# Writing a relative-bias table to DRAM as 8 copies of each row instead of 128, and reading it back with sixteen loads of eight partitions

## The chip, the cores and the metric

One core of a Trainium2 chip runs the whole program. The metric is the device time of one execution in microseconds (us). The core's engines are TensorE (PE, with its weight loads listed apart as PEld), VectorE (DVE), ScalarE (ACT), GpSimd (POOL) and SyncE (SP). Each runs its own list of instructions in order and waits on semaphores. SP and POOL also issue DMAs: those of SP stand in the profile's queue q1, those of POOL in q0. Both queues' packets are carried by the same 16 DMA engines.

## The reference, cut to what matters

The program is a decoder trunk of two layers on 256 tokens of width 1024. A layer is a feed-forward half-step (gate, up, silu, down), a mixing step with three kinds of attention, and a second feed-forward half-step. Each step is modulated by vectors that come from a conditioning vector `c` and a large weight `w_ada`. All arithmetic is float32, and every weight matrix is read from HBM once.

What matters here is the bias that two of the attention kinds add to their scores. For each of 12 heads it depends only on the distance of query and key:

```python
def band_bias(table_cols, dilation):
    rel = jnp.arange(BLK)[:, None] + BLK - jnp.arange(2 * BLK)[None, :]
    b = t5_bucket(jnp.maximum(rel, 0) * dilation)
    return jnp.transpose(table_cols[b], (2, 0, 1)).astype(jnp.float32)
...
    s = jnp.einsum('nbqhgd,nbkhd->nbhgqk', qb, kk) * (Dh ** -0.5) + bias
```

So for a head, row p of the 128 x 256 bias block is the same vector of 383 distances, read from a start that moves one place to the left with each row: T[p, k] = row[127 - p + k].

## The kernel before, in words

**Order of the work.** The program is a list of units in an order fixed by hand: first feed-forward step (stage s=0), mixing step (s=1), feed-forward (s=2), and the same for the second layer (s=3 to 5). A unit is a piece of weight of 128 x 1024 float32. It is loaded into a `raw` tile of 1 MB that holds two units (L133, three such tiles), split by ACT into a high part `wH` (L150) and by DVE into a low part `wL` (L158), and then used by PE in three products for each piece: high x high, low x high, high x low (L594 for the products `pf`, `pq`, `pg`; L706 for the rows `pd` and `pe` of the down product). Six `wH` and six `wL` tiles exist. `feed()` prepares units up to five ahead of the one that PE is at.

**The modulation vectors.** Woven between the units is a second stream: `w_ada` pieces of 512 KB (tile `ada`, L260, two tiles), each multiplied by a scalar per partition and added to an accumulator `acc` (L281 on ACT for the first of eight, L283 on DVE for the others). Its pace per unit is set by the table `PACE`; the chunks that the next stage needs are completed at that stage's end. A load of a new piece is issued by SP only when the piece two before it has been consumed, and DVE runs the `acc` and `wL` instructions in one order.

**End of a feed-forward step.** The last four units of the down product are run half by half of the columns (L736 to L761); after each half DVE adds the result to `x` (`y` L535, `x` L536), then follow the mean square (`jk` L452), the root on POOL (`r` L466, L467), the scaled `xn` (L475) and the transposes `psn` (L488) that start the next stage. In the mixing step the first products are `pv` (L942).

**The bias table.** `bias_loads` (L413) fetches a one-hot matrix, a mask `mk` and the 32 x 12 table early in stage 0. `bias_table` (L425), called after unit 16 of that stage, makes `mk`, the 12 rows of 383 values, with one matmul (L428) and one DVE addition (L429). It stores them to DRAM as `row` (L431), and with a DMA from DRAM to DRAM writes each row 128 times into `scr` (L433). `load_bias` (L435), called at the start of each of the two mixing steps (L1149), reads from `scr` with one DMA the whole 128 x 12 x 256 tile `T` (in the profile `Tm`, since it lies in a larger tile of that name): the stride of 382 between partitions makes the moving start. T is first used at L1054, by the additions of the dilated heads.

Of the kernel before, what the change touches and what calls it, by code (L numbers as in the profile page):

```python
# [10 lines left out]
F32 = mybir.dt.float32  # L11
# [5 lines left out]
P = 128  # L17
# [6 lines left out]
NHEAD = 12  # L24
NDIST = 383
# [64 lines left out]
class Trunk:  # L90
# [334 lines left out]
    def bias_table(self):  # L425
        nc, oh, mk, rb = self.nc, self.oh, self.mk, self.rb
        p = self.ps("psr")
        nc.tensor.matmul(p[:NHEAD, :NDIST], rb, oh, start=True, stop=True)  # L428
        nc.vector.tensor_tensor(mk, p[:NHEAD, :NDIST], mk, op=ALU.add)  # L429
        row = self.dp.tile([NHEAD, NDIST], F32, tag="row", name="row")  # L430
        nc.gpsimd.dma_start(row, mk)  # L431
        self.scr = self.dp.tile([NHEAD, P, NDIST], F32, tag="scr", name="scr")
        nc.gpsimd.dma_start(self.scr, row.unsqueeze(1).to_broadcast([NHEAD, P, NDIST]))  # L433

    def load_bias(self, T):  # L435
        base = self.scr[:, 0:P, 0:256]
        src = bass.AP(tensor=base.tensor, offset=base.offset + P - 1,
                      ap=[[NDIST - 1, P], [P * NDIST, NHEAD], [1, 256]])
        self.nc.gpsimd.dma_start(T, src)


    def square(self, t, cols, tag):
# [908 lines left out]
```

## Time and profile before

| | |
|---|---|
| median of 3 runs | 1211.04 us (1210.54 to 1213.16) |
| the profiled execution | 1215.12 us, of which the span of its instructions is 1213.4 us |
| PE busy | 1181.0 us, 97% of the span |
| DVE busy | 837.3 us, 69% |
| ACT busy | 616.0 us, 51% |
| POOL busy | 19.0 us, 2% |
| moved by DMA | 287.55 MB, mean 237 GB/s |

The busy times say that PE has work at nearly every moment, but a matmul that waits inside its pipeline or runs at half clock counts as busy too. What matters for a change in the DMAs is where PE, and the chain of work that ends last, waits for data; that is read from the chain in order of time and from tables by stretch, which stand below the diff.

### The profile page before, as it was taken

To read this page: it belongs to the slowest core of one execution; us is meant where nothing else is said; L and a number is where in the kernel's file an instruction comes from. 1 tells how busy PE (TensorE), PEld (TensorE's weight loads), DVE (VectorE), ACT (ScalarE), POOL (GpSimd) and SP (SyncE) were. 2 spreads that over 40 slices of the span, in tenths; PEclk is the share of its full clock that TensorE was granted. 3 is DMA by queue.
4 is the path that set the end of the run, shared out by engine and by line. 5 is a ranking of instruction groups with operands and counts; after the bars stand their busy time and mean duration, and the time that the engine had idled before them with its cause. 6 is when DMAs were issued, how large, how long until landed. Compare 5 with 4: busy or idle time off the path is not lost.

```text
span 1213.4 us, 21101 instructions
## 1 busy us (share of the span) xinstructions
PE 1181.0 (97%) x8765; PEld 1102.9 (91%) x8765; DVE 837.3 (69%) x1087; ACT 616.0 (51%) x953; POOL 19.0 (2%) x38
## 2 busy tenths in 40 slices
PE   6999998899999999999999999999999999999997
PEld 5999986699999899999889999889999998999986
DVE  3677575878889888766577666567766788555544
ACT  5555343556555475444365444346655456444432
POOL 1000000000000000000000000000000000000000
PEclk9999999899999999999999999999999999999999
DMA  9999889698769959876738676748743584556550
GB/s 318 313 303 332 272 308 318 211 314 271 253 230 314 319 176 326 263 243 242 261 112 298 219 242 226 258 157 291 264 149 113 186 276 147 190 178 197 180 176 35
DMA packets 189671, 287.55 MB, mean 237 GB/s; under 512 B 6806, under 2 KB 155496, under 8 KB 189576
## 3 DMA queue, kind: packets, MB, share of 16 engines
q1 hardware_dynamic: 187656, 279.88, 68.8%
q0 software_dynamic: 1776, 6.14, 1.7%
q8 instruction: 68, 1.11, 0.4%
q14 instruction: 27, 0.22, 0.1%
q10 hardware_dynamic: 144, 0.20, 0.0%
HBM read 285.12 MB, written 3.42 MB: 238 GB/s over the span
## 4 chain that ended last, share of the span: by engine, by line
PE 85%; DMA 6%; DVE 3%; ACT 2%; issue 2%; POOL 1%; SPq 0%; POOLq 0%; ACTq 0%; DVEq 0%
PE pf L594 37%; PE pd L706 16%; PE pg L594 12%; PE pq L594 7%; DMA ada<-in_w_ada 5%; PE pb L594 3%; PE pf L624 3%; PE pv L942 2%; DVE acc L283 1%; DVE wL L158 1%; PE adaf L212 1%; DMA first<-in_w_ada 1%; PE psn L488 1%; ACT wH L150 1%; ACT jk L452 0%
## 5 line engine op out<-in xcount | busy, mean ns | idle before, releaser
L158 DVE TENSOR_TENSOR wL<-raw,wH 128x1024 fp32r<-128x1024 f32 (+1 forms) x384 | 461.8, 1211 | 224.8 <-ACT wH L150 224.3
L150 ACT CAST wH<-raw 128x1024 fp32r<-128x1024 f32 (+1 forms) x384 | 393.1, 1040 | 244.5 <-PE pd L706 90.1
L594 PE MATMUL pf<-hH,wH 128*128 128x256 f32 x1312 | 324.5, 285 | 0.4 <-DVE hH L505 0.4
L594 PE MATMUL pf<-hH,wL 128*128 128x256 f32 x1312 | 323.5, 284 | 0.0
L594 PEld LDWEIGHTS pf<-hH,wH 128*128 128x128 f32 x1312 | 253.1, 193 | 1.7 <-issue 0.9
L594 PEld LDWEIGHTS pf<-hH,wL 128*128 128x128 f32 x1312 | 253.5, 193 | 0.2 <-issue 0.2
L594 PE MATMUL pf<-hL,wH 128*128 128x256 f32 x1312 | 183.8, 283 | 0.0
L283 DVE SCALAR_TENSOR_TENSOR acc<-ada,sc,acc 128x1024 f32<-128x1024 f32 x112 | 143.4, 1280 | 40.6 <-DMA ada<-in_w_ada 40.6
L594 PEld LDWEIGHTS pf<-hL,wH 128*128 128x128 f32 x1312 | 169.1, 192 | 0.0
L706 PE MATMUL pd<-wL,ffH 128*128 128x512 f32 x336 | 132.7, 395 | 5.1 <-DVE wL L158 5.1
L706 PE MATMUL pd<-wH,ffH 128*128 128x512 f32 x336 | 132.5, 394 | 0.0
L706 PE MATMUL pd<-wH,ffL 128*128 128x512 f32 x336 | 132.2, 393 | 0.0
L594 PE MATMUL pg<-hH,wH 128*128 128x256 f32 x384 | 96.0, 288 | 0.0
L594 PE MATMUL pg<-hH,wL 128*128 128x256 f32 x384 | 94.0, 283 | 0.0
L652 ACT ACTIVATE sil<-pf 128x256 f32<-128x256 f32 x88 | 33.3, 382 | 98.4 <-PE pf L594 98.4
L706 PEld LDWEIGHTS pd<-wL,ffH 128*128 128x128 f32 x336 | 63.9, 190 | 19.3 <-DVE wL L158 6.2
L706 PEld LDWEIGHTS pd<-wH,ffH 128*128 128x128 f32 x336 | 63.9, 190 | 14.0 <-issue 0.8
L706 PEld LDWEIGHTS pd<-wH,ffL 128*128 128x128 f32 x336 | 64.0, 190 | 13.2
L594 PEld LDWEIGHTS pg<-hH,wH 128*128 128x128 f32 x384 | 73.5, 191 | 2.3 <-issue 0.9
L594 PEld LDWEIGHTS pg<-hH,wL 128*128 128x128 f32 x384 | 73.6, 192 | 0.0
L653 DVE TENSOR_TENSOR f<-pf,sil 128x256 f32<-128x256 f32 x88 | 36.9, 422 | 33.9 <-ACT sil L652 33.9
L594 PE MATMUL pq<-hH,wH 128*128 128x256 f32 x224 | 55.8, 287 | 0.0
(215 smaller groups left out, 1437.2 us busy)
## 6 DMA issues: line engine op xcount, KB each, us to landing
ada<-in_w_ada SPq DMA_DIRECT2D x128, 512.0 KB, 5.4
raw<-in_w_ffn_down SPq DMA_DIRECT2D x44, 1024.0 KB, 4.8
raw<-in_w_in SPq DMA_DIRECT2D x42, 1024.0 KB, 6.1
raw<-in_w_ffn_gate SPq DMA_DIRECT2D x41, 1024.0 KB, 6.1
raw<-in_w_ffn_up SPq DMA_DIRECT2D x41, 1024.0 KB, 5.8
first<-in_w_ada SPq DMA_DIRECT2D x32, 256.0 KB, 6.0
raw<-in_w_out SPq DMA_DIRECT2D x8, 1024.0 KB, 7.1
raw<-in_w_ffn_gate SPq DMA_DIRECT2D x12, 256.0 KB, 6.0
```

Source lines behind the costliest of these rows:

```text
L150: nc.scalar.copy(u.H, u.view(self.raw_tiles[u.raw]))
L158: nc.vector.tensor_tensor(u.L, u.view(self.raw_tiles[u.raw]), u.H, op=ALU.subtract)
L212: self.nc.tensor.matmul(self.first_ps[q % 2][32 * i:32 * i + 32, 0:P], w, src[:, i * P:(i + 1) * P], start=kb in (0, None), stop=kb == KB - 1)
L283: self.nc.vector.scalar_tensor_tensor(acc, src, sc, acc, ALU.mult, ALU.add)
L488: self.nc.tensor.transpose(p[:, i * P:(i + 1) * P], xn[:, fb * P:(fb + 1) * P], self.ident)
L594: nc.tensor.matmul(out, w[:, kb, cs], x[:, kb, :], start=i == 0, stop=i == n - 1)
L624: self.nc.tensor.matmul(ps[fb][:, S * up:S * up + S], w[:, 2 * k + up, b * P:(b + 1) * P], x[:, 2 * q + k, :], start=q == 0 and not up and ...
L652: nc.scalar.activation(sil, p[:, :S], AF.Silu)
L653: nc.vector.tensor_tensor(f32, p[:, S:], sil, op=ALU.mult)
L706: self.nc.tensor.matmul(out, x[:, kb, sl], w[:, 0, hs], start=first and i == 0, stop=last and i == 2)
L942: self.nc.tensor.matmul(out, x[:, 4 * (i % 2) + k, sl], w[:, k, :], start=i % 2 == 0 and j == 0, stop=i % 2 == 1 and j == n - 1)
```

## The change

The table `scr` gets 8 copies of each row instead of 128. They are written by eight DMAs straight from `mk` in SBUF, one for each copy, and the DRAM tile `row` with its store goes. T is read by sixteen DMAs of eight partitions each instead of one of 128: copy i serves partition r + i, and the start of each load moves with r. The same bytes of T arrive, 1.5 MB for each of the two mixing steps; all DMAs concerned are issued by POOL before and after. The lines below the edit move by two (L439 becomes L441, L1054 becomes L1056).

```diff
--- before.py
+++ after.py
@@ -427,16 +427,18 @@
         p = self.ps("psr")
         nc.tensor.matmul(p[:NHEAD, :NDIST], rb, oh, start=True, stop=True)
         nc.vector.tensor_tensor(mk, p[:NHEAD, :NDIST], mk, op=ALU.add)
-        row = self.dp.tile([NHEAD, NDIST], F32, tag="row", name="row")
-        nc.gpsimd.dma_start(row, mk)
-        self.scr = self.dp.tile([NHEAD, P, NDIST], F32, tag="scr", name="scr")
-        nc.gpsimd.dma_start(self.scr, row.unsqueeze(1).to_broadcast([NHEAD, P, NDIST]))
+        self.scr = self.dp.tile([NHEAD, 8, NDIST], F32, tag="scr", name="scr")
+        for r in range(8):
+            nc.gpsimd.dma_start(self.scr[:, r, :], mk)
 
     def load_bias(self, T):
-        base = self.scr[:, 0:P, 0:256]
-        src = bass.AP(tensor=base.tensor, offset=base.offset + P - 1,
-                      ap=[[NDIST - 1, P], [P * NDIST, NHEAD], [1, 256]])
-        self.nc.gpsimd.dma_start(T, src)
+
+
+        for r in range(0, P, 8):
+            base = self.scr[:, 0:8, 0:256]
+            src = bass.AP(tensor=base.tensor, offset=base.offset + P - 1 - r,
+                          ap=[[NDIST - 1, 8], [8 * NDIST, NHEAD], [1, 256]])
+            self.nc.gpsimd.dma_start(T[r:r + 8], src)
```

The order on POOL, from the table to the first read of T, before the change. `r` are the roots of the norms, and the names in brackets are the semaphores that a row waits for (DMASW0 to DMASW7 are the eight that POOL's DMAs take in turn, DMAHW0 to 7 those of SP's):

```order
L431 DMA row<-mk 12x383 [waits DVE_49]
L433 DMA scr<-row 1536x1x383 [waits DMASW3_49]
L466 TENSOR_TENSOR r_0_2311<-ms_0_2287 128x1 [waits DVE_49,Activation_49]
L467 TENSOR_TENSOR r_0_2311<-r_0_2311,mhalf 128x1 [waits Pool_49]
L467 TENSOR_TENSOR r_1_2427<-r_1_2427,mhalf 128x1 [waits DVE_49]
L439 DMA Tm_2485<-scr 128x12x256 [waits DMAHW3_49,DMAHW4_49,DMAHW2_49,DMAHW5_49,DMAHW1_49,DMAHW6_49,DMAHW0_49,DMAHW7_49,DMASW4_49,PE_49]
```

The same place after it; of the last eight loads of T the first two stand here, and the other six differ only in the semaphore's number:

```order
L432 DMA scr<-mk 12x383 [waits DVE_49]
L432 DMA scr<-mk 12x383 x4
L432 DMA scr<-mk 12x383 [waits DMASW0_49]
L432 DMA scr<-mk 12x383 [waits DMASW1_49]
L432 DMA scr<-mk 12x383 [waits DMASW2_49]
L468 TENSOR_TENSOR r_0_2316<-ms_0_2292 128x1 [waits DVE_49,Activation_49]
L469 TENSOR_TENSOR r_0_2316<-r_0_2316,mhalf 128x1 [waits Pool_49]
L469 TENSOR_TENSOR r_1_2432<-r_1_2432,mhalf 128x1 [waits DVE_49]
L441 DMA Tm_2490<-scr 8x12x256 [waits DMAHW0_49,DMASW7_49,DMAHW1_49,DMASW6_49,DMAHW2_49,DMASW5_49,DMAHW3_49,DMASW4_49,DMAHW4_49,DMASW3_49,DMAHW5_49,DMASW2_49,DMAHW6_49,DMASW1_49,DMAHW7_49,DMASW0_49,PE_49]
L441 DMA Tm_2490<-scr 8x12x256 x7
L441 DMA Tm_2490<-scr 8x12x256 [waits DMASW3_49]
L441 DMA Tm_2490<-scr 8x12x256 [waits DMASW4_49]
```

The wait of the copying DMA for `row` is gone, and no compute instruction of POOL has changed its place. Of the sixteen loads of T eight can be in flight; each of the others waits until an earlier one has landed and freed its semaphore.

On DVE the first use of T in the first mixing step stood as follows before, with one semaphore for T:

```order
L283 SCALAR_TENSOR_TENSOR acc_1_2889<-ada_3108,sc,acc_1_2889 128x1024 [waits DMAHW3_49,DVE_49]
L1054 SCALAR_TENSOR_TENSOR p_dil_3224<-pa_dil_3215,Tm_2485 128x2x256 [waits DMASW5_49,PE_49]
L1054 SCALAR_TENSOR_TENSOR p_dil_3224<-pb_dil_3216,Tm_2485 128x256
L1054 SCALAR_TENSOR_TENSOR p_dil_3224<-pc_dil_3217,Tm_2485 128x2x128 [waits PE_49]
L1054 SCALAR_TENSOR_TENSOR p_dil_3224<-pb_dil_3216,Tm_2485 128x128
```

And after the change, with eight:

```order
L283 SCALAR_TENSOR_TENSOR acc_1_2909<-ada_3128,sc,acc_1_2909 128x1024 [waits DMAHW3_49,DVE_49]
L1056 SCALAR_TENSOR_TENSOR p_dil_3244<-pa_dil_3235,Tm_2490 128x2x256 [waits DMASW4_49,DMASW3_49,DMASW5_49,DMASW2_49,DMASW6_49,DMASW1_49,DMASW7_49,DMASW0_49,PE_49]
L1056 SCALAR_TENSOR_TENSOR p_dil_3244<-pb_dil_3236,Tm_2490 128x256
L1056 SCALAR_TENSOR_TENSOR p_dil_3244<-pc_dil_3237,Tm_2490 128x2x128 [waits PE_49]
L1056 SCALAR_TENSOR_TENSOR p_dil_3244<-pb_dil_3236,Tm_2490 128x128
```

Its place among DVE's instructions is unchanged. The same eight semaphores in place of one are waited for at two instructions near the end of stage 0, a `y` (L535) and the second half of an `xn` (L478), which take over the buffer of `mk` once it has been read.

## Rows read from the trace of the kernel before

**Rows 1.** The chain that ended last, share of the span by engine.
```profile
PE 85%; DMA 6%; DVE 3%; ACT 2%; issue 2%; POOL 1%; SPq 0%; POOLq 0%; ACTq 0%; DVEq 0%
```

**Rows 2.** That chain in order of time, 118 to 242: start us, us, what.
```profile
124.33 19.39 DMA ada<-in_w_ada
...
151.40 1.28 DVE acc L283
...
163.04 1.29 DVE acc L283
...
164.34 8.55 DMA ada<-in_w_ada
...
222.44 0.61 DVE y L535
```

**Rows 3.** PE in order of time: start us, us, operation [idle before <-releaser].
```profile
213.57 0.80 PE L706 MATMUL pd<-wL,ffH 128*128 128x512 f32 x1 [4.41 <-DVE wL L158]
...
215.90 0.79 PE L706 MATMUL pd<-wL,ffH 128*128 128x512 f32 x1 [0.68 <-DVE wL L158]
...
227.99 1.27 PE L488 MATMUL psn<-ident,xn 128*128 128x128 f32 x8 [1.35 <-ACT xn L475]
```

**Rows 4.** Stretches: us, busy (instructions) of each engine, PEclk, DMA share, GB/s.
```profile
100.00:116.00 16.00, 16.00 (x130) 15.23 (x129) 10.88 (x13) 7.55 (x10) 0.57 (x1) 1.00 1.02 351
120.00:140.00 20.00, 20.00 (x164) 19.52 (x163) 11.64 (x16) 6.45 (x10) 0.00 (x0) 1.00 0.96 260
140.00:155.00 15.00, 15.00 (x127) 15.00 (x126) 10.19 (x13) 6.56 (x10) 0.00 (x0) 1.00 0.79 290
160.00:216.00 56.00, 50.10 (x227) 39.15 (x226) 36.86 (x36) 19.87 (x22) 0.00 (x0) 0.96 0.91 314
211.50:221.80 10.30, 7.55 (x17) 5.49 (x18) 7.34 (x7) 2.08 (x2) 0.00 (x0) 0.50 0.93 293
236.00:242.00 6.00, 4.83 (x33) 4.21 (x34) 5.72 (x12) 6.00 (x12) 0.00 (x0) 1.00 0.82 262
244.00:260.00 16.00, 16.00 (x135) 16.00 (x135) 12.22 (x13) 8.58 (x12) 0.00 (x0) 1.00 1.00 326
1011.70:1016.50 4.80, 3.02 (x14) 1.47 (x13) 3.08 (x8) 3.44 (x9) 1.19 (x2) 1.00 0.12 45
1017.00:1020.50 3.50, 3.50 (x18) 3.50 (x18) 3.47 (x9) 3.50 (x8) 0.00 (x0) 0.51 0.13 48
```

**Rows 5.** DMA queues between 120 and 140: packets, MB, share of 16 engines.
```profile
q1 hardware_dynamic: 1525, 2.82, 49.6%
q0 software_dynamic: 703, 2.36, 45.4%
```

**Rows 6.** DMA issues over the span: count, KB each, median us to landing.
```profile
ada<-in_w_ada SPq DMA_DIRECT2D x128, 512.0 KB, 5.4
...
Tm<-scr POOLq DMA_DIRECT2D x2, 1536.0 KB, 7.8
...
scr<-row POOLq DMA_DIRECT2D x1, 2298.0 KB, 24.1
...
row<-mk POOLq DMA_DIRECT2D x1, 18.0 KB, 4.8
```

**Rows 7.** Who ACT waited for, 97 to 131: us in total, times, longest.
```profile
ACT wH L150 <- PE pf L594: 8.8, 5, 2.6
```

**Rows 8.** Line 431, and line 439: ns min/median/max, first and last start.
```profile
L431 POOL DMA_DIRECT2D row<-mk x1: 568/568/568, 111.2 to 111.2; - x1
...
L439 POOLq EVENT_SEMAPHORE  x6: 17/43/43, 233.4 to 817.4; - x6
L439 POOL DMA_DIRECT2D Tm<-scr x2: 1088/1142/1197, 234.3 to 817.9; - x2
```

**Rows 9.** First users of T, 300 to 310 and 890 to 905, same columns.
```profile
L1054 DVE SCALAR_TENSOR_TENSOR p_dil<-pa_dil,Tm x1: 682/682/682, 307.0 to 307.0; 128x512 f32<-128x512 f32 x1
...
L1054 DVE SCALAR_TENSOR_TENSOR p_dil<-pa_dil,Tm x2: 676/684/692, 890.6 to 899.6; 128x512 f32<-128x512 f32 x2
```

## The prediction

> **What bounds the kernel now.** I read the chain of work that ended last first. It is PE for 85% and DMA for 6% [rows 1], so a change in DMAs counts only where that 6% lies. In order of time the chain is PE until about 124 us, then leaves it for a hundred: from 124.33 it goes through loads of `ada` pieces and the DVE instructions that consume them (19.39 us, later 8.55 us, and others of that kind) until DVE's `y` at 222.44 starts the norm of the next stage [rows 2]. After that it is PE again up to the end. The reader is to see that one load which takes 5.4 us in the median [rows 6] took 19.39 here, and that it was issued at 124.33, eight us after POOL issued the table's copy.
>
> The second view is the table by stretch. Between 100 and 116 the DMAs move 351 GB/s at a full share; between 120 and 140 they move 260 GB/s at almost the same share [rows 4]. The queues tell why: in those 20 us q0, the copy to `scr`, took 45.4% of the engines for 2.36 MB, and q1, which carries every weight, got 2.82 MB [rows 5], that is 141 GB/s. The copy took 24.1 us to land [rows 6].
>
> The third view is who pays for it. Up to 131 ACT's casts of new units wait for PE to free a tile (8.8 us in five waits) [rows 7]: the weight stream is ahead as far as its buffers let it. PE does not stop during the copy (busy 20.00 of 20) [rows 4]; it lives on what is buffered. [...] Together 4.41 + 0.68 + 1.35 + 3.8 = 10.2 us, the most that PE itself can get back in this stage. In the second layer no such copy exists, so nothing is to be had there.
>
> **The copy that goes.** In 120 to 140 the stream would have gone on at least at the 290 GB/s of the next 15 us and at most at the 351 of the 16 before [rows 4]: 5.8 to 7.0 MB in place of 2.82, so 3.0 to 4.2 MB are missing. At the 314 GB/s of 160 to 216 [rows 4] these take 9.5 to 13.4 us to make good. Not all of it need reach the end: between 151.40 and 163.04 the chain holds no DMA, DVE works off its backlog [rows 2], and part of the delay is caught up there; and without the copy the stream cannot run further ahead than its tiles. But from 160 to 216 the DMAs have a share of 0.91 [rows 4], so the stream goes at their pace, and a lead that exists at 160 stays until the end. Bounds: 0 (all was caught up) and 10.2 (what PE can use). I take 9.5, near the upper end, since it is the smaller of the two counts by bytes and the wait at 213.57 shows that the delay was still there.
>
> **What is late next.** With the waits gone, PE reaches the end of the stage up to 10.2 us earlier, the DVE chain to `psn` only 9.5, so the wait before `psn` grows from 1.35 to about 2 us. At 1011.7 to 1016.5 PE was busy 3.02 of 4.80 us, and from 1017 the granted clock was 0.51 for 3.5 us, which costs half of that, 1.75 [rows 4]. At 226 to 228, with 1.35 us idle, it stayed up. The new idle lies between the two. After `psn` PE is on the chain, so such a drop would cost what it now hides. I take off 1.5 us (between 0 and two such drops, 3.5).
>
> **The eight writes.** Eight POOL issues of 0.57 us, as for `row<-mk` [rows 8], are 4.6 us in place of 0.57 + 1.1 and the wait for `row` between. The next instruction of POOL is a root at 226, so they are hidden; the cover is a hundred us. They carry 8 x 18 KB, 0.15 MB in place of 2.36, which at 314 GB/s is 0.5 us of stream; I count it within the rounding of the 9.5.
>
> **The sixteen reads of T.** One load of 1.5 MB landed 7.8 us after its issue [rows 6], in a gap of the weight stream (82% share, 262 GB/s between 236 and 242) [rows 4]. Now there are sixteen issues on POOL, 0.57 us each by `row<-mk` or 1.1 by the old load [rows 8], 9 to 18 us; behind them in POOL's list stand only the roots of the next stage. None of the trace's loads has eight partitions. If eight in flight behave as the old load did, two rounds take 2 x 7.8 = 16 us; if each waited for the one ahead and took 7.8, 125 us. T is first used at 307.0 and at 890.6 [rows 9], 72.7 us after the issues at 234.3 and 817.9 [rows 8]. So the bounds are 0 and 52 us in each mixing step, and they decide at 4.5 us for each load if fully serial. I take 0: eight semaphores let them overlap, and a small POOL transfer landed in 4.8 [rows 6], so the likely total is 15 to 25 us. A gain isn't to be had, since nobody waits for T now.
>
> **The added waits.** Seven more semaphores at each of four instructions (`y`, `xn`, and two first users of T). A semaphore row costs 17 to 43 ns [rows 8], so 14 of them at `y` and `xn`, on the chain, cost 0.2 to 0.6 us; I take 0.3. The two users of T run beside PE.
>
> **The sum.** 9.5 - 1.5 - 0.3 = 7.7 us. The profiled execution took 1215.12 us for a span of 1213.4, 4.1 above the median of 1211.04; I take the same difference off the median: 1203.3 us.
>
> **The rivals.**
>
> *Most of the delay was caught up, and the clock takes the rest.* The lead that the tiles can hold is small, so the stream without the copy is held back by PE until 155, and the stretch after it needs more than the DMAs give; then 3 to 5 us of the 9.5 are left, less 1.5 for the clock. For it: the 11.6 us without a DMA in the chain at 151 to 163 [rows 2]. Against it: the DMAs were below full at 140 to 155 (0.79) [rows 4], so time was lost there that an undisturbed stream would use. Price: a gain of about 2.7, 1208.3 us.
>
> *The copy is hidden anyway.* PE's waits at 213 come from the demand of the last units and the `ada` chunk, and would stand without the copy. For it: PE never stopped between 120 and 155 [rows 4]. Against it: the casts waited for PE before 131 [rows 7], and the load of 124 took 19 us [rows 2]. Price: 0, 1211 us.
>
> *The pieces of T choke the weights.* Eight neighbouring partitions are a narrow target, and a slow T holds up DMA engines that the weights need, as the copy did. From 244 to 260 the weights run at 326 GB/s with a full share [rows 4], so there is no room. The copy took 4.2 MB from q1 at most for its 2.36; T at the same exchange takes 2.8 MB each, 8.6 us at 326, and twice that in all, 17.2. If the buffers absorb nothing, that is 17.2 - 7.7 = 9.5 us slower, 1220.5. It decides from 45% of that toll on (7.7 of 17.2). For it: the copy shows that POOL traffic can halve the weight stream. Against it: the old T ran at 262 GB/s, and T is now spread over a time in which PE has tiles in hand.
>
> [...]
>
> **How the numbers follow.** Forecast 0.64, with its own range 1200.5 (all 10.2 and no clock drop) to 1206.5. The first rival 0.18, the hidden copy 0.10, the choked weights 0.08. About 0.2%, 2.4 us, is what a measurement of this kernel tells from no change. Faster takes the 0.64 and most of the first rival, 0.15: 0.79, and a little of the last where the toll is small, 0.01: 0.80. The same: 0.03 of the first and 0.10 of the second, 0.13. Slower: 0.07. For 8 times in 10 the range runs from 1200 to 1209: it holds the forecast's own and the first rival.
>
> **What would show it.** Right: the loads of `ada` issued near 124 land in 5 to 9 us; 120 to 140 shows about 300 GB/s; the two `wL` waits of `pd` are gone or below 1 us; the clock is full at 211; `y` at about 213 instead of 222.44, `psn` near 220, and from there every row of PE earlier by the same 7 to 8 us. T lands within 30 us, and no wait of DVE for it at 299 or 883. Wrong: `y` comes at 219 or later although q1 ran at 300 GB/s; or PE waits for `wL` between 240 and 300 or 825 and 890, which it does not now; or a half-clock stretch sits right behind `psn` for 10 us.

## The result: slower by 0.63%

| | before | after |
|---|---|---|
| median | 1211.12 us (1210.54 to 1213.16, 4 runs) | 1219.87 us (1218.08 to 1222.48, 4 runs) |
| profiled execution, its span | 1215.12, 1213.4 us | 1218.08, 1216.4 us |

The ratio after to before is 1.0063, 95% interval 1.0051 to 1.0076, that is 6.2 to 9.2 us; the two medians lie 8.75 us apart. The prediction was 1203.3 us with a range from 1200 to 1209: wrong in sign. The mechanism of the third rival, the choked weights at 1220.5, is what the profile shows.

Beware of the two profiles: they differ by only 3.0 us, since the one of before is an execution 4 us above its median and the one of after the quickest of its four. Differences between them are read by place, and sizes from the medians.

The chain that ended last, share of the span by engine, after the change. It answers [rows 1]:

```profile
PE 81%; DMA 9%; DVE 3%; ACT 3%; issue 2%; POOL 0%; SPq 0%; POOLq 0%; ACTq 0%; DVEq 0%
```

DMA's share rose from 6 to 9%. Where it lies is in the chain in order of time (start us, us, what), which answers [rows 2]:

```profile
206.86 4.94 DMA ada<-in_w_ada
...
220.72 1.73 PE psn L490 x8
...
238.64 16.09 DMA raw<-in_w_in
...
260.83 5.75 DMA ada<-in_w_ada
...
267.99 4.91 DMA ada<-in_w_ada
...
274.30 6.40 DMA ada<-in_w_ada
...
284.24 1.19 PE pc L994 x2
```

The long load of stage 0 is gone, and `psn` starts at 220.72 instead of 227.99. But the chain now leaves PE a second time, in the first mixing step: a weight load (`raw`) issued at 238.64 takes 16.09 us, the `ada` loads behind it are issued late, and PE waits for a DVE result (`e`) that stands behind their `acc` in DVE's order. PE's waits over the whole span (us in total, times, longest), answering [rows 3]:

```profile
PE pc L994 <- DVE e L988: 6.5, 1, 6.5
...
PE psn L490 <- ACT xn L477: 4.5, 1, 4.5
...
PE po L1010 <- ACT z L1001: 1.0, 1, 1.0
```

The two `wL` waits of `pd` near 214 are gone; the 6.5 us for `e` are new. DVE's own waits between 236 and 290 say which load is behind them. Before:

```profile
DVE acc L283 <- DMA ada<-in_w_ada: 7.9, 4, 3.4
DVE wL L158 <- ACT wH L150: 4.2, 7, 1.5
```

After:

```profile
DVE wL L158 <- ACT wH L150: 12.7, 3, 9.2
DVE acc L283 <- DMA ada<-in_w_ada: 7.8, 4, 2.4
```

DVE waits as long for `ada` as before. What grew, by 8.5 us, is its wait for `wH`, the cast of the weights that landed late.

Now the stretches, with the columns of [rows 4] (us, busy and instructions of PE, PEld, DVE, ACT, POOL, then PEclk, DMA share, GB/s):

```profile
120.00:140.00 20.00, 20.00 (x166) 19.76 (x165) 15.17 (x19) 8.14 (x12) 0.00 (x0) 1.00 0.75 258
211.50:221.80 10.30, 5.76 (x34) 4.88 (x33) 9.06 (x16) 5.39 (x10) 1.10 (x2) 0.98 0.90 291
221.30:224.70 3.40, 3.40 (x15) 3.17 (x15) 1.76 (x7) 3.11 (x9) 0.00 (x0) 0.51 0.00 1
231.00:236.00 5.00, 3.84 (x27) 3.26 (x27) 4.72 (x9) 5.00 (x10) 4.35 (x9) 1.00 1.10 118
240.00:250.00 10.00, 10.00 (x86) 10.00 (x85) 2.08 (x2) 0.00 (x0) 0.12 (x1) 1.00 1.08 169
276.00:282.80 6.80, 1.77 (x15) 1.56 (x14) 4.79 (x8) 4.27 (x5) 0.00 (x0) 1.00 0.88 295
282.80:289.60 6.80, 5.36 (x21) 5.02 (x22) 4.95 (x9) 6.11 (x9) 0.00 (x0) 0.50 0.87 298
```

Read it from the top. Between 120 and 140 the DMAs are no longer full (0.75 in place of 0.96). The half-clock stretch of 10.3 us at 211.5 is gone; a shorter one stands behind the start of `psn`. From 231 on the DMA engines are more than full (a share of 1.10: the times of the packets add up to more than the sixteen engines have) and move 118 GB/s: those are the pieces of T, as the queues of those 5 us show below. Between 240 and 250 they are still full at 169 GB/s, where before the share of 1.00 moved 326 from 244 on [rows 4]. At 276 to 282.8 PE is nearly idle, and right behind it its clock is granted at 0.50 for 6.8 us. PE was busy 5.36 of those. Its `pq` matmuls start 0.21 us apart there, from 288.21 on, and 0.12 us apart from 289.67 on, at a clock of 1.00; by that ratio the clock took about 2.4 us on top of the wait, an estimate.

DMA queues between 231 and 236 (packets, MB, share of 16 engines), then the loads of T and of weights between 225 and 256 (count, KB each, median us to landing), answering [rows 6]:

```profile
q0 software_dynamic: 355, 0.59, 109.8%
...
raw<-in_w_in SPq DMA_DIRECT2D x4, 1024.0 KB, 13.7
Tm<-scr POOLq DMA_DIRECT2D x16, 96.0 KB, 6.8
```

Only q0, T's queue, is at work in those 5 us: 0.59 MB takes the whole of sixteen engines for 5.5 us. Before, the same view of 225 to 256 had:

```profile
raw<-in_w_in SPq DMA_DIRECT2D x5, 1024.0 KB, 5.8
Tm<-scr POOLq DMA_DIRECT2D x1, 1536.0 KB, 7.7
```

A piece of a sixteenth of the size lands hardly sooner than the whole T did, and the weights behind it take 13.7 us in place of 5.8. The sixteen issues run from 228.6 to 239.5, the last piece lands at 250.8:

```profile
L441 POOL DMA_DIRECT2D Tm<-scr x16: 579/579/690, 228.6 to 239.5; - x16
...
DMA to landing us min/median/max: 4.2/6.8/11.3
```

The first weight load is issued at 236.4. Before, T was issued at 234.3, landed 7.7 us later, and the first weight load went out at 242.1: the old T just fitted into the gap.

The account by place, from the starts of four PE groups in both profiles (`psn` of stage 1, `pz`, the first `pa_dil`, the same of the second layer):

| stretch | before | after | difference |
|---|---|---|---|
| start to `psn` | 227.99 | 220.72 | -7.3 |
| `psn` to `pz` | 41.85 | 43.39 | +1.5 |
| `pz` to `pa_dil` | 34.42 | 43.64 | +9.2 |
| second layer, `psn` to `pa_dil` | 76.62 | 77.84 | +1.2 |

In the second layer the three weight loads behind T take 13.9 to 15.3 us as well, yet PE loses only the 1.0 us in front of `po`. The first `ada` load of the step is issued 11.6 us later against `psn` in the first layer and 8.0 us later in the second, so the second has some 7 us of room and the first some 5. Why the rooms differ I did not try. The sum, +4.7 before rounding, is 1.7 us above 3.0; that fits the half-clock stretch at 1017, which the profile of before has [rows 4] and that of after doesn't: its `pf` matmuls start 0.22 us apart, and 0.12 us right behind it at a clock of 1.00, so it cost about 1.6 of its 3.50 us, an estimate.

### The profile page after: what moved, and what is told of

It reads as the page before. It is cut to its first block, busy times and chain, and to the rows that moved or that the text cites. A ratio compares the mean times of both kernels' runs of the same rounds, so it can differ in the third digit from the quotient of the medians.

```text
span 1216.4 us, 21153 instructions
## 1 busy us (share of the span) xinstructions
PE 1180.2 (97%) x8765; PEld 1103.2 (91%) x8765; DVE 837.1 (69%) x1087; ACT 615.6 (51%) x953; POOL 37.7 (3%) x74
## 4 chain that ended last, share of the span: by engine, by line
PE 81%; DMA 9%; DVE 3%; ACT 3%; issue 2%; POOL 0%; SPq 0%; POOLq 0%; ACTq 0%; DVEq 0%
PE pf L596 39%; PE pd L708 17%; PE pg L596 12%; DMA ada<-in_w_ada 4%; DMA raw<-in_w_in 3%; PE pb L596 3%; PE pf L626 2%; PE pq L596 1%; DMA first<-in_w_ada 1%; DVE wL L158 1%; ACT wH L150 1%; DVE acc L283 1%; PE psn L490 1%; PE pe L708 1%; PE adag L344 1%
## 5 line engine op out<-in xcount | busy, mean ns | idle before, releaser
L708 PEld LDWEIGHTS pd<-wH,ffH 128*128 128x128 f32 x336 | 63.1, 188 | 13.7 <-issue 0.8
```

Source lines behind the costliest of these rows:

```text
L708: self.nc.tensor.matmul(out, x[:, kb, sl], w[:, 0, hs], start=first and i == 0, stop=last and i == 2)
```

## The experiments

There are two sets of runs, and each is compared with its own runs of the kernel before: median 1212.08 us (23 runs) for e1 to e4, 1212.82 (26 runs) for e5 to e8. Differences in us are those of the medians.

**e5, the eight writes alone.** T is read with the bytes and strides of before the change, but out of a weight matrix, so it holds no bias values.

```diff
 (from after)
-        for r in range(0, P, 8):
-            base = self.scr[:, 0:8, 0:256]
-            ... ap=[[NDIST - 1, 8], [8 * NDIST, NHEAD], [1, 256]])
-            self.nc.gpsimd.dma_start(T[r:r + 8], src)
+        base = self.a["w_in"][0]
+        ... ap=[[NDIST - 1, P], [P * NDIST, NHEAD], [1, 256]])
+        self.nc.gpsimd.dma_start(T, src)
```

> The eight writes of the change are kept and the large copy is gone, and T is read by one load with the strides of the kernel before, but out of the tensor in_w_in, since 128 copies no longer exist; the bias values are then other ones. It prices the write side alone, with a read that is as good as before's (in e1 a read of one single copy was slow: 13.8 us). Theory (the copy's removal is worth several us when T costs nothing): faster than before by 3 to 8 us, T lands within 8 us, raws behind it in 5 to 7. Rival (the lighter write is worth about the 0.9 us that e1 showed, since most executions of before lose little at the end of the first stage): within 2.4 us of before.

Measured: 1209.36 us (11 runs), ratio 0.9970 [0.9959, 0.9981], 3.5 us faster. After the program's start PE's only long wait is the 4.7 us before `psn`, and the weight loads behind T land in 5.2 and 5.9 us:

```profile
PE psn L487 <- ACT xn L474: 4.7, 1, 4.7
...
DMA to landing us min/median/max: 5.2/5.6/5.9
```

So the write side alone is a gain, about half of the 7.7 that I forecast.

**e2, the sixteen reads alone.** The write side is that of before (row, then 128 copies), and the loads of eight partitions take each row from its own copy.

```diff
 (from before)
-                      ap=[[NDIST - 1, P], [P * NDIST, NHEAD], [1, 256]])
-        self.nc.gpsimd.dma_start(T, src)
+        for r in range(0, P, 8):
+            ... offset=base.offset + P - 1 + r * (NDIST - 1),
+                ap=[[NDIST - 1, 8], [P * NDIST, NHEAD], [1, 256]])
+            self.nc.gpsimd.dma_start(T[r:r + 8], src)
```

> The write side is that of the kernel before (row, then 128 copies), only the read of T is in sixteen loads of eight neighbouring partitions, each from its own eight copies. Theory (narrow destination): T arrives at 100 to 107 GB/s as in the changed kernel, the raw loads of in_w_in behind it take 13 to 16 us, PE waits some 6 us before the pc matmuls of the first mixing step and about 1 us in the second: 8 to 14 us slower than before. Rival (all loads read the same 147 KB of HBM, and that place is the narrow one): here they read different copies, T arrives at over 200 GB/s and the time is within 2.4 us of before.

Measured: 1224.10 us (5 runs), ratio 1.0097 [1.0083, 1.0112], 12.0 us slower. From 236 to 239 T arrives at 99 GB/s, and the two weight loads behind it take 13.3 and 15.7 us, close to the theory.

```profile
PE pc L993 <- DVE e L987: 7.4, 1, 7.4
...
PE pd L707 <- DVE wL L158: 2.9, 2, 1.5
```

The waits of before (`wL`) and of after (`e`) stand side by side, and -3.5 and +12.0 add to +8.5 where the whole change gave +8.75 (7.6 by its ratio). Within these intervals the two halves add up, and for loads of eight neighbours the source, 8 copies or 128, doesn't matter: the loads themselves cost the time.

**e1, the table of eight copies, read by one load.** All 128 partitions are read out of one copy, from a start that moves by one element.

```diff
 (from after)
-        for r in range(0, P, 8): ... ap=[[NDIST - 1, 8], [8 * NDIST, NHEAD], [1, 256]])
+        src = bass.AP(tensor=base.tensor, offset=base.offset,
+                      ap=[[1, P], [8 * NDIST, NHEAD], [1, 256]])
+        self.nc.gpsimd.dma_start(T, src)
```

> The eight writes of the change are kept, but T is read with one DMA of 128 partitions as before. The moving start of T runs the wrong way here (plus one place per row in place of minus one), so the bias values differ; bytes, packets and instructions are those of a single load. Theory (the narrow loads of T are the whole loss, and the write side brings what the prediction's 9.5 - 1.5 said): faster than the kernel before by 4 to 9 us; psn starts near 220.7 as in the changed kernel (227.99 before); T lands within 8 us; the raw loads behind it land in 5 to 7 us; no wait of PE for e near 277. Rival (the pulled-forward first stage itself upsets the mixing step, for instance by its half-clock stretch at 221): the loss of some 11 us in the mixing step stays, and the time is at or above 1215.

Measured: 1211.18 us (12 runs), ratio 0.9992 [0.9982, 1.0002]. Neither the theory's 4 to 9 us nor the rival's 1215 came: the loss is gone, and so is most of the gain. T took 13.6 us in the median of its two loads, and the weight loads behind it 8.1 to 9.0:

```profile
Tm<-scr POOLq DMA_DIRECT2D x2, 1536.0 KB, 13.6
```

One wide load isn't quick by its width alone; I had expected it to be as the old one. Which property of the source slows it is open, since e5 with the wide strides took 8.0.

**e3 and e8, the same sixteen loads on other partitions.** Each load takes every sixteenth partition. In e3 their order jumps by four, in e8 it is 0, 1, 2, and so on.

```diff
 (from after)
-        for r in range(0, P, 8):
+        for r in (0, 4, 8, 12, 1, 5, 9, 13, 2, 6, 10, 14, 3, 7, 11, 15):   # e8: range(16)
...
-                          ap=[[NDIST - 1, 8], [8 * NDIST, NHEAD], [1, 256]])
-            self.nc.gpsimd.dma_start(T[r:r + 8], src)
+                          ap=[[NDIST - 16, 8], [8 * NDIST, NHEAD], [1, 256]])
+            self.nc.gpsimd.dma_start(T[r:P:16], src)
```

> As the changed kernel, eight copies and sixteen loads of eight partitions on POOL, but a load takes every sixteenth partition in place of eight neighbours, and loads that follow each other lie four partitions apart. [...] Rival (sixteen separate DMAs with eight partitions each are slow by their number and their semaphores): T arrives at 100 to 107 GB/s as in the changed kernel, 1217 to 1222 us.

> As e3 (eight copies, sixteen loads of every sixteenth partition), but issued in the order 0, 1, 2, 3 and so on, so that loads in flight together lie on neighbouring partitions. [...] Rival (spreading a load over the partitions is enough): as e3, 1209 to 1212.

Measured: e3 1211.10 us (11 runs), ratio 0.9987 [0.9978, 0.9995]; e8 1214.93 us (10 runs), 1.0019 [1.0006, 1.0033]. Bytes, packets' sizes, count of loads and POOL's issues are those of after; what differs is which partitions are written at one time, and which places of `scr` are read at one time. q0 and landing in e3, between 231 and 239:

```profile
q0 software_dynamic: 674, 1.02, 49.3%
...
Tm<-scr POOLq DMA_DIRECT2D x14, 96.0 KB, 3.1
```

and in e8, between 231 and 237, with PE's wait there:

```profile
q0 software_dynamic: 475, 0.76, 90.1%
...
Tm<-scr POOLq DMA_DIRECT2D x11, 96.0 KB, 5.3
```

```profile
PE pc L992 <- DVE e L986: 4.2, 1, 4.2
```

In e3 a piece lands in 3.1 us and T leaves half of the engines free; PE doesn't wait for `e` in the mixing step. POOL's sixteen issues of 0.58 us draw T out: the last is at 240.1, and the weight loads issued at 239.1 and 241.4 land in 9.2 and 9.7 us. In e8 neighbours follow each other, and 3.1 us of the 9.7 between e3 and the changed kernel are back: its 1214.93 us lie above the 1209 to 1212 that its rival gave, and its +2.1 us against before lie between e3's -1.0 and the changed kernel's +8.75. So eight partitions to a load are not the loss as such, as e3 shows; it came with pieces that follow each other on neighbouring partitions. The order also changes what is read together: starts in `scr` one element apart in e8, four in e3. The four loads of e6 below start one element apart too and are quick (1.57 MB in 6 us), so I put the difference down to the partitions; e8 alone doesn't separate the two.

Why neighbouring partitions are slow together no run shows, nor how many pieces moved at one time.

**e6 and e7, 32 copies by one DMA, and four loads of 32 partitions.** e6 takes every fourth partition per load, e7 32 neighbours. In both T holds the bias values of before.

```diff
 (from after)
-        self.scr = self.dp.tile([NHEAD, 8, NDIST], F32, tag="scr", name="scr")
-        for r in range(8):
-            nc.gpsimd.dma_start(self.scr[:, r, :], mk)
+        self.scr = self.dp.tile([NHEAD, 32, NDIST], F32, tag="scr", name="scr")
+        nc.gpsimd.dma_start(self.scr, mk.unsqueeze(1).to_broadcast([NHEAD, 32, NDIST]))
...
+        for r in range(4):                          # e7: range(0, P, 32), NDIST - 1, T[r:r + 32]
+            ... ap=[[NDIST - 4, 32], [32 * NDIST, NHEAD], [1, 256]])
+            self.nc.gpsimd.dma_start(T[r:P:4], src)
```

> 32 copies, written by one DMA from SBUF (0.59 MB), and T read by four loads of 32 partitions, each taking every fourth one. [...] Rival (POOL's queue of several loads is what costs): 1213 or more.

> As e6, with 32 neighbouring partitions for each load in place of every fourth. [...] Rival (only the number of partitions in a load counts): the same T as in e6 within 1 us.

Measured: e6 1208.69 us (9 runs), ratio 0.9966 [0.9952, 0.9979]; e7 1208.16 us (7 runs), 0.9957 [0.9942, 0.9972]. Both beat the kernel before and the changed one, by 4.1 and 4.7 us against before; between the two the intervals overlap. q0 in e6 from 229 to 235, and in e7 from 231 to 237:

```profile
q0 software_dynamic: 448, 1.57, 82.2%
```

```profile
q0 software_dynamic: 320, 1.18, 94.8%
```

In e6 all of T goes through in those 6 us. In e7 the four loads need 10.6 us, and its weight loads, issued from 238.2 on, land in 5.3 and 6.0, as in e6: the rest of T is small enough by then. That the spread of e6 is the quicker T shows in the rows; in the time it doesn't, and I take it that the gap before the weights hides either.

**e4, before once more.** No edit, the profile of another execution.

> The kernel before, unchanged, for a second profile. The profiled execution of before took 1215.1 us against a median of 1211. Theory (PE's wait of 4.4 us and the half-clock stretch of 10 us near 212 are at home in every execution): a span of about 1209 to 1213 in which both still stand. Rival (they were a mishap of that one profile, and the usual execution has less to gain from a lighter copy): a span near 1209.5, in which PE's waits for wL near 212 are under 2 us or the clock stays up.

Measured: 1213.81 us (span 1212.1). It has the same wait for `wL`, nearly as long in sum (5.1 us before), and the half-clock stretch, here from 214 to 219 (columns of [rows 4]):

```profile
PE pd L706 <- DVE wL L158: 4.8, 2, 3.5
...
214.00:219.00 5.00, 4.99 (x12) 3.93 (x13) 2.42 (x2) 1.25 (x2) 0.00 (x0) 0.50 0.93 284
```

The theory holds for it, but this execution too lies above the median.

From the table's matmul (`psr`) to `psn` the three profiles with the 2.36 MB copy took 118.5 (before), 117.0 (e4) and 114.5 us (e2); the seven without took 111.0 to 113.1. The means are 116.6 and 111.9. So up to `psn` the copy cost 4.7 us on average and 6.6 in the one execution that I had; three profiles with it are few.

**All together.** Multiply q0's share by the length of its window and divide by its MB, and take that for the 1.57 MB of T: it is an estimate of how long T holds all sixteen engines.

| kernel | q0 in its window | T holds the engines | us against before |
|---|---|---|---|
| e6 | 6 us, 82.2%, 1.57 MB | 4.9 us | -4.1 |
| e5 | 6 us, 82.9%, 1.52 MB | 5.1 us | -3.5 |
| e3 | 8 us, 49.3%, 1.02 MB | 6.1 us | -1.0 |
| e7 | 6 us, 94.8%, 1.18 MB | 7.6 us | -4.7 |
| e1 | 8 us, 76.3%, 1.21 MB | 7.9 us | -0.9 |
| e8 | 6 us, 90.1%, 0.76 MB | 11.2 us | +2.1 |
| after | 5 us, 109.8%, 0.59 MB | 14.6 us | +8.75 |

The gap between T's first issue and the first weight load is 7.8 us before and after, and 7.6 to 8.6 in the other profiles (8.6 in e1). Every kernel whose T holds the engines for less than its gap is faster or the same; the two above it are slower, and the one further above is the slower. e2, whose large copy is still there, comes to 16.4 us by the same sum (3 us, 104.3%, 0.30 MB), and its reads cost 12.0. e3 and e1 gain less than e5; POOL's issues and the slow source may be why, but no run separates that.

## Why the prediction was wrong

- **"The sixteen reads of T", taken as 0.** This is the step that failed. I asked whether T would be there at its own use 72 us later, and it was: DVE never waited for it, and "15 to 25 us" came out at 22. But the price of these loads was what they took from the queue beside them: weight loads of 13.7 us in place of 5.8. The row on which it turned was in the groups: the stretch of 236 to 242 with a share of 0.82 [rows 4] was the last free stretch before the weights resumed at full share, and the old T filled it to the end. The cost is 12 us by e2, and after's own profile places 9.2 of it between `pz` and `pa_dil`: 6.5 of waiting and some 2.4 of half clock.
- **The third rival, with 0.08.** Its mechanism (pieces of T hold up the weights) is shown by e2, e3 and e8, and its time of 1220.5 is 0.6 us off. That the time came so close is in part luck: the sum took 8.6 us in each layer, and the toll was 9.2 in the first and 1.2 in the second, with a smaller gain (3.5, not 7.7) to set against it. I held against it that the old T had run at 262 GB/s and that T was now spread out; both said nothing of narrow loads, which no row of before showed. To the rival's narrow target I gave no number of its own: its toll came from the copy.
- **"The copy that goes", taken as 9.5.** Right mechanism, wrong size. I filled 120 to 140 with 290 to 351 GB/s; it showed 258 at a share of 0.75, 5.15 MB on q1 in place of 2.82. The stream waits for tiles there, as the first rival said: ACT stands 6.3 us for PE to free a `wH`. Against that rival I had held the share of 0.79 at 140 to 155; but without the copy the share is no higher at 120 to 140, so a share below full is no sure sign of time lost to it. 2.3 MB at 314 GB/s are 7.4 us, and the two profiles differ by 7.3 at `psn`. The rest is the execution that I had: by the means of ten profiles 4.7, and in the time 3.5 by e5. I had seen that it lay 4.1 us above the median, and subtracted that from the time but not from the gain, although the wait that I was pricing is one of the things that vary (5.1, 4.8 and 2.9 us in the three profiles with the copy).
- **The 3.8 us for the clock in the 10.2.** No run shows this term as it stands. Before, `pd` matmuls start 0.43 us apart from 216.49 to 221.19, where the granted clock is 0.50, and 0.23 us apart from 204.69 to 208.77, where it is 1.00; by that ratio the clock took about 3.5 of the 7.55 us [rows 4], an estimate, and the 10.2 become 10.0. The 9.5 that I took lies below both.
- **"What is late next", -1.5.** The cost came as forecast: a half-clock stretch of 3.4 us at 221.3 and 1.5 us more between `psn` and `pz`. But e4 has such a stretch behind its `psn` too (43.27 us from `psn` to `pz`), so before pays it as well in some executions, and it is no sure cost of the change. The wait before `psn` itself was forecast at about 2 us and is 4.5.
- **"The eight writes" and "the added waits".** The writes land in 5.1 us each in the median, and e5, which has them, is faster; I see no cost of the writes. From `psr` to `psn` e6 and e7 with their single copying DMA took 111.0 and 112.2 us, the kernels with eight writes 111.1 to 113.1. The added waits no run separates.
- **What I named as signs.** `ada` loads near 124 in 5 to 9 us (4.6 in the median from 120 to 140), no `wL` wait at 213, full clock at 211, `psn` near 220: these came. `y` came at 215.1, not 213. About 300 GB/s between 120 and 140 did not come, it was 258. The sign of failure that I gave, PE waiting for `wL` between 240 and 300, came in another form: `e` behind late `ada` loads. A slip in the numbers changes nothing: a gain of 10.2 ends at 1200.8, not at 1200.5.

## What to carry to other kernels

When a transfer is split, don't ask only when its own reader needs it: find which stream next uses the DMA engines, and compare the gap before it (7.8 us here) with how long the new pieces hold the engines (14.6 us here; share times time per MB, not GB/s). Try the same bytes in wider or more widely spread pieces: here four loads of 32 partitions with 32 copies kept the whole gain of the smaller table (-4.1 and -4.7 us), sixteen of eight neighbours turned it into a loss (+8.75). And before a gain is sized from a wait in one execution that lies above its median, expect it to be smaller in others: here 4.7 us on average up to `psn` where the first profile showed 6.6.

## What the runs showed that I had not expected

- Eight neighbouring partitions per load: 118 GB/s at a share of 1.10, while the same bytes with partitions sixteen apart went at 128 with a share of 0.49. A share of 1.00 before had moved 326 [rows 4], so the share here said nothing of the bytes moved, and the weight loads of the other queue went from 5.8 to 13.7 us.
- The order of the loads alone, 0, 4, 8, 12 against 0, 1, 2, 3, changed their landing from 3.1 to 5.3 us and the kernel by 0.3% (ratios 0.9987 and 1.0019, intervals apart).
- One load of 128 partitions out of a single copy of 12 x 383 values took 13.6 us, against 8.0 out of a large matrix with the old strides.
- An issue of one of the sixteen loads took POOL 0.58 us, and the sixteen ran from 228.6 to 239.5: longer than the 7.7 us in which the wide load landed.
